# An encoder block on one core: modulation sums spread over the input projection, whose VectorE, ScalarE and GpSimd work runs in written order, and value products of an attention unit in one row

## The chip, the cores and the metric

One core of a Trainium2 chip runs the whole kernel in one launch. The metric is device time in microseconds (us); smaller is better. Below, TensorE (PE) is the matrix engine, VectorE (DVE), ScalarE (ACT) and GpSimd (POOL) work on tiles, and SyncE (SP) issues most DMAs.

## The reference, cut to what matters

A block of 1024 tokens by 1024 channels, float32. Six modulation vectors come from `c`. The mixing half scales and shifts a normalised `x`, multiplies it by one input projection, mixes the first 512 columns with a 2-D Fourier transform, runs windowed attention on the rest (8 query heads, 2 key/value heads, blocks of 128 queries that see the block before, their own and the next one) and projects back. The channel half is a mixture of 16 experts, each on its 128 best tokens.

```python
mod = jnp.einsum('bd,de->be', silu(c), w_ada) + b_ada
sh1, sc1, g1, sh2, sc2, g2 = split(mod, 6)
h = rmsnorm(x, norm_mix_g) * (1.0 + sc1) + sh1
u_f, q, k, v = split(h @ w_in)
q, k = rmsnorm(q, q_norm_g), rmsnorm(k, k_norm_g)
x = x + g1 * (concat([fourier_mix(u_f), windowed_gqa(q, k, v, rel_bias, sink)]) @ w_out)
h2 = rmsnorm(x, norm_ffn_g) * (1.0 + sc2) + sh2
x = x + g2 * expert_choice_moe(h2)
```

## The kernel before, in words

Products are float32 made of three reduced-precision ones: a value is split into a high part (ScalarE copy, L79) and a low part (VectorE subtraction, L80), and TensorE multiplies high by high, low by high and high by low.

**Input projection (L314 to L537).** The 1024 tokens are eight tiles of 128. Tiles 0 and 1 go together while the weights arrive; their order is written out by `in_order(t0, *PINNED)` (L469), which ties each instruction of an engine to the one written before it. Tiles 2 to 7 follow in the loop over `seq` (L493): twelve stages, two for a tile, each of four input chunks. One chunk is `project`: three terms of two or four matmuls (L367). At the head of a stage `chunk` (L258) makes the scaled, transposed and split input of the next stage: four PE transposes (L264), four ScalarE activations (L271, tile `hf`), the split into `hh` (L79) and `hl` (L80). At the head of a tile's first stage also: `scale_x` of the next tile (L222, ScalarE, needs `xr`), and `norm_x` of the tile after that (square on ScalarE L186, a small VectorE operation L187, a power on GpSimd L189 that gives `xr`). Here nothing ties the order of an engine: the compiler's list scheduler orders the instructions by its own estimate of when each is ready.

After a tile's last product `finish` (L374) copies the results out of PSUM (`qn` on VectorE L377; `kk`, `vf`, `un` on ScalarE L378 to L380) and appends the generator `qknorm` (L278) to a list. After each chunk `bg_tick` (L351) advances every `qknorm` by one step: squares (L280, L281), a sum and a scaling on VectorE (L283, L284) and a power on GpSimd (L286, `qr`); two steps later four GpSimd products (L290, L292, L295 twice: `qn`, `kk`, `kd`); four steps later two PE transposes (L302) and a split into `khi` and `klo`.

`bg_tick` also advances `ada_parts` (L140): four of the six modulation vectors, each as eight weighted sums over rows of `w_ada` on VectorE (L114, L116, tile `ws`, one a step), then two matmuls that add over partitions (L174), then a bias (L176); its loads go through SP (L148), its stores through GpSimd's DMA queue (L154). From the second stage on, every other chunk advances it once more (L529), which makes 1.5 steps a chunk. PSUM tiles `pt` (two buffers) serve the chunk transposes, L302 and L174 alike.

**Attention (L540 to L1016).** Sixteen units (tile, key/value head) run through `qprep`, `front` (logits L677 and L678, bias and maximum L680, exponentials L689, division L695) and `back` (L698). `back` handles the unit's two or three key blocks one by one: `flip_p` transposes the probabilities of a block (four PE transposes, L706) and copies them to SBUF (ScalarE L708, tile `pT`, `PB` = 2 buffers); then two value products go into the halves of a PSUM tile (L719, tile `yp`). Each block's transposes are made one block ahead, and between the blocks `tick` advances a filler: first the Fourier group, later the output projection (L74 to L76). The order of all engines is again the list scheduler's.

**Selection and experts (from L1020).** Tokens are chosen on VectorE and TensorE, then the experts' products run back to back, in written order.

Of the kernel before, what the change touches and what calls it, by code (L numbers as in the profile page):

```python
# [30 lines left out]
PINNED = ("PE", "DVE", "Activation", "Pool", "SP")  # L31
RAW1, RAW2, RAW3 = 4, 5, 4
SCRATCH = 4096
SB, PB, WB, YB = 9, 2, 4, 3
OLD = NT - 2
NSW, RATE1, RATE2 = 5, 2.0, 1.3
TK = 3
# [8 lines left out]
def block_kernel(ctx: ExitStack, tc: tile.TileContext, t_in, out):  # L46
    nc = tc.nc
    PE, ACT, DVE, POOL, SP = nc.tensor, nc.scalar, nc.vector, nc.gpsimd, nc.sync
# [7 lines left out]
    def pool(name, bufs=1, space=None, **kw):  # L56
        if space is None:
            return tc.tile_pool(name=name, bufs=bufs, reuse_waits="tile", **kw)
        return tc.tile_pool(name=name, bufs=bufs, space=space, **kw)
# [6 lines left out]
    def pt(name="pt"):  # L66
        return ps.tile([128, 512], F32, name=name, tag="pt", bufs=2)
# [10 lines left out]
    def split(hi, lo, src, eng=None):  # L78
        ACT.activation(hi, src, AF.Copy)  # L79
        return (eng or DVE).tensor_tensor(lo, src, hi.bitcast(F32), op=OP.subtract)  # L80
# [41 lines left out]
    def traced():  # L122
        return len(nc.cur_bb.bb.instructions)

    def in_order(start, *engines):
        last = {}
        for i in list(nc.cur_bb.bb.instructions)[start:]:
            e = str(i.engine).split(".")[-1]
            if e in engines:
                if e in last:  # L130
                    tc.add_manual_dep(i, last[e].name, NOSYNC, reason="program order")
                last[e] = i

    def drain(g):
        for _ in g:
            pass
# [46 lines left out]
    def rms(pool_, src, name, tag, bufs, eng=None):  # L183
        junk = pool_.tile([128, D], BF, name="junk", tag=tag, bufs=bufs)
        ss = pool_.tile([128, 1], F32, name=name + "s", bufs=3)
        ACT.activation(junk, src, AF.Square, accum_out=ss)  # L186
        (eng or DVE).tensor_scalar(ss, ss, 1.0 / D, EPS, op0=OP.mult, op1=OP.add)  # L187
        rs = pool_.tile([128, 1], F32, name=name + "r", bufs=3)
        POOL.tensor_tensor(rs, ss, mhalf[:, 0:1], op=OP.pow)  # L189
        return rs  # L190
# [23 lines left out]
    def load_x(t):  # L214
        xs[t] = p1.tile([128, D], F32, name="xt", bufs=4)
        SP.dma_start(xs[t], x[t * 128:(t + 1) * 128, :])

    def norm_x(t):
        xr[t] = rms(p1, xs[t], "x", tag="hf", bufs=2)

    def scale_x(t):
        ACT.activation(xs[t], xs[t], AF.Copy, scale=xr.pop(t))  # L222
# [53 lines left out]
    px_ = [pt]  # L276

    def qknorm(t, kk):  # L278
        q_n = qn[t]
        ACT.activation(sq[:, 512:], kk, AF.Square)  # L280
        ACT.activation(sq[:, :512], q_n, AF.Square)  # L281
        qs = ust.tile([128, 10], F32, name="qs", bufs=2)
        DVE.tensor_reduce(qs, sq.rearrange("p (h d) -> p h d", d=64), axis=AX.X, op=OP.add)  # L283
        DVE.tensor_scalar(qs, qs, 1.0 / HD, EPS, op0=OP.mult, op1=OP.add)  # L284
        qr = ust.tile([128, 10], F32, name="qr", bufs=2)
        POOL.tensor_tensor(qr, qs, mhalf[:, :10], op=OP.pow)  # L286
        yield
        yield
        qv = q_n.rearrange("p (h d) -> p h d", d=64)
        POOL.tensor_tensor(qv, qv, qr[:, :8, None].to_broadcast([128, 8, 64]), op=OP.mult)  # L290
        kv_ = kk.rearrange("p (h d) -> p h d", d=64)
        POOL.tensor_tensor(kv_, kv_, qr[:, 8:10, None].to_broadcast([128, 2, 64]), op=OP.mult)  # L292
        kd = ust.tile([128, 2, 2, 64], F32, name="kd", bufs=2)
        for dup in range(2):
            POOL.tensor_tensor(kd[:, :, dup, :], kv_, gg[:, None, :].to_broadcast([128, 2, 64]), op=OP.mult)  # L295
        yield
        yield
        yield
        yield
        p = px_[0]()  # L300
        for kv in range(2):
            PE.transpose(p[:, kv * 128:kv * 128 + 128], kd[:, kv].rearrange("p a d -> p (a d)"), ident)  # L302
        split(khi[:, :, t * 128:t * 128 + 128], klo[:, :, t * 128:t * 128 + 128],
              p[:, :256].rearrange("p (a b) -> p a b", b=128))
# [44 lines left out]
    bg, ada, dfts = [], [], []  # L349
# [10 lines left out]
    def terms(ts, kc, hs_, o):  # L360
        for l, r in ((0, w_h), (1, w_h), (0, w_l)):
            for s_ in range(len(ts)):
                lhs = hs_[l][:, o + s_ * 128:o + s_ * 128 + 128]
                for acc, c0, c1 in zip(accs[s_], (0, 512, 1024), (512, 1024, 1280)):

                    first = kc == 0 and l == 0 and r is w_h and not (s_ and c0 == 1024)
                    PE.matmul(acc[:, :c1 - c0], lhs, r[kc][:, c0:c1], start=first, stop=(kc == 7 and r is w_l),  # L367
                              skip_group_check=c0 == 1024)
            yield

    def project(ts, kc, hs_, o):
        drain(terms(ts, kc, hs_, o))
# [79 lines left out]
    pair_products(4, 6)  # L452
    norm_x(2)
    norm_x(3)
    project(pair, 6, hs.pop(6), 0)
    scale_x(2)
    nxt = chunk((2,), 0, 4)
# [32 lines left out]
        folded.append(fold(j, u_n[j], u_n[j + 4]))  # L490

    seq = [(t, kc) for t in range(2, NT) for kc in (0, 4)]
    for m, (t, kc0) in enumerate(seq):  # L493
        hs_ = nxt
        if m == len(seq) - 1:
            for g in ada:
                drain(g)
            p_w.close()
            pfs.append(p_f.enter_context(pool("pf", side="right")))
            for n, wid in ((4, 512), (2, 256), (1, 128), (1, 128)):  # L500
                basis(n, wid)
        if kc0 == 0:
            if t == 2:
                load_x(4)
            if t + 3 < NT:
                load_x(t + 3)
            if t + 1 < NT:
                scale_x(t + 1)
            if t + 2 < NT:
                norm_x(t + 2)  # L510
            accs = [[pu(), pu(), (px, pv)[t % 2]()]]
        if m + 1 < len(seq):
            nxt = chunk((seq[m + 1][0],), seq[m + 1][1], 4)
        for a in range(4):
            project((t,), kc0 + a, hs_, a * 128)
            if m == 0 and a == 1:
                DVE.scalar_tensor_tensor(gg, qg, HD ** -0.5, kg, op0=OP.mult, op1=OP.mult)
                p = pt()
                PE.matmul(p[:8], rb, oh, start=True, stop=True)
                DVE.tensor_tensor(brow, p[:8], brow, op=OP.add)  # L520
            if m == 1 and a == 0:
                SP.dma_start(bd, brow)
            if m == 1 and a == 1:
                SP.dma_start(bd2, bd[None, :, :].to_broadcast([128, 8, 512]))
            if m or a > 1:
                bg_tick()
            if m == len(seq) - 1 and a < 3:
                level0(a)
            if m > 0 and a % 2:  # L529
                next(ada[0], None)  # L530
        if kc0 == 4:
            finish(0, t)
    for g in bg[:-1]:
        drain(g)
    for g in bg[-1:]:
        next(g)
    p_a.close()  # L537


# [158 lines left out]
    def back(t, kv):  # L698
        blocks = span(t)
        sbs = fr.pop((t, kv))  # L700
        yp = ypb()

        def flip_p(bi):
            pp = pt()
            for s_, i in enumerate((0, 2, 1, 3)):
                PE.transpose(pp[:, s_ * 128:s_ * 128 + 128], sbs[i][:, bi * 128:bi * 128 + 128], ident)  # L706
            pT = pb.tile([128, 512], F32, name="pT", bufs=PB)
            ACT.activation(pT, pp, AF.Copy)  # L708
            return pT

        nxt = flip_p(0)
        for bi, b in enumerate(blocks):
            yield
            pT = nxt
            if bi + 1 < len(blocks):
                nxt = flip_p(bi + 1)
            tick()
            for par in range(2):
                PE.matmul(yp[par * 64:par * 64 + 64, :256], vf[:, b, kv * 64:kv * 64 + 64],  # L719
                          pT[:, par * 256:par * 256 + 256], start=(bi == 0), stop=(bi == len(blocks) - 1))  # L720
        ypv = yp[:, :256].rearrange("p (a b) -> p a b", b=128)
        if po is None:
            ya = pb.tile([128, 2, 128], F32, name="ya", bufs=2)
            ACT.activation(ya, ypv, AF.Copy)
            SP.dma_start(yda[t][:, kv * 2:kv * 2 + 2, :], ya)
            ydone[t, kv] = None
        else:
            while ylive[0] >= YB:
                next(fill[0])
            h, l = ysplit(t, kv)  # L730
            split(h, l, ypv)
            ydone[t, kv] = h, l
# [217 lines left out]
    def tick():  # L950
        debt[0] += rate[0]
        while debt[0] >= 1.0:
            debt[0] -= 1.0
            next(fill[0], None)
# [459 lines left out]
```

## Time and profile before

| what | value |
| --- | --- |
| median of 3 runs | 1017.39 us (1016.72 to 1017.52) |
| the profiled execution's own time | 1017.5 us |
| its span, first to last instruction | 1015.4 us |
| TensorE busy | 958.8 us, 94% |
| VectorE, ScalarE, GpSimd busy | 787.4, 628.0, 403.8 us |
| TensorE's share of the chain that ended last | 83% |

The span lies 2.1 us under the execution's own time. Busy time of TensorE is modelled from pipelined records; where an engine stands still, the profile names what ended the wait. In views of stages, the columns give busy time and the number of instructions of each engine, then the mean granted clock of TensorE (1.00 is 2.4 GHz, 0.50 is 1.2 GHz), the share of time in which the DMA engines were busy, and GB/s.

### The profile page before, as it was taken

Reading aid. Unit: us, or ns where it says so; the run is one execution under the profiler, and the core shown is the slowest. Engines: PE = TensorE matmul, PEld = TensorE weight load, DVE = VectorE, ACT = ScalarE, POOL = GpSimd, SP = SyncE. Lnnn points to the kernel's source line nnn. Section 1 sums busy time; section 2 is a strip of 40 time slices with the busy share of each in tenths; the row PEclk is TensorE's granted clock in tenths of the full one; section 3 lists DMA queues with packets and bytes.
Section 4 is the critical chain, followed back from the end, with each engine's and each line's share of the span. In section 5 each row is a group of like instructions: output and inputs, shape, how many; then the busy total and the mean of one; then the engine's idle time right before and its main releaser. Section 6 shows DMA issues by size and latency. Waiting matters only on the chain.

```text
span 1015.4 us, 13138 instructions
## 1 busy us (share of the span) xinstructions
PE 958.8 (94%) x4737; PEld 747.6 (74%) x4737; DVE 787.4 (78%) x1240; ACT 628.0 (62%) x832; POOL 403.8 (40%) x236
## 2 busy tenths in 40 slices
PE   4997999979999999599899999999999999999996
PEld 3676877756777777458788888888888888888884
DVE  1346865777666869779869888988988898899894
ACT  2473444666455553226667777777777777777772
POOL 0026453100000000000357669768776876782203
PEclk9998999989999999599999999999999999999998
DMA  9966664361222138889989999999999999999912
GB/s 292 337 231 248 253 266 126 97 201 53 87 80 73 54 139 304 319 324 352 374 309 385 378 376 411 381 379 399 390 377 379 411 377 380 390 397 379 380 60 41
DMA packets 91641, 283.95 MB, mean 280 GB/s; under 512 B 8140, under 2 KB 25728, under 8 KB 91448
## 3 DMA queue, kind: packets, MB, share of 16 engines
q1 hardware_dynamic: 86712, 266.32, 69.3%
q0 software_dynamic: 4864, 16.80, 6.5%
q8 instruction: 37, 0.61, 0.2%
q14 instruction: 28, 0.23, 0.1%
HBM read 263.79 MB, written 21.40 MB: 281 GB/s over the span
## 4 chain that ended last, share of the span: by engine, by line
PE 83%; DVE 6%; POOL 3%; issue 2%; ACT 2%; DMA 1%; SPq 1%; POOLq 0%; ACTq 0%; DVEq 0%
PE pa L74 17%; PE pa L75 17%; PE pa L76 16%; PE pu L367 5%; PE pt L1258 3%; PE yp L719 3%; PE pj L75 2%; PE pj L74 2%; PE pa L1217 2%; PE pj L76 2%; PE pt L706 2%; PE pt L829 2%; PE lg L677 1%; DVE ws L116 1%; PE lg L678 1%
## 5 line engine op out<-in xcount | busy, mean ns | idle before, releaser
L80 DVE TENSOR_TENSOR wl<-raw,wh 128x2048 fp32r<-128x2048 f32 (+1 forms) x189 | 423.3, 2267 | 64.4 <-ACT wh L79 62.9
L79 ACT ACTIVATE wh<-raw 128x2048 fp32r<-128x2048 f32 (+1 forms) x189 | 355.7, 1895 | 79.0 <-PE pa L75 73.9
L1231 POOL TENSOR_SCALAR oneh<-tri_f,pos 128x128 bf16<-128x128 f32 x96 | 210.3, 2206 | 15.2 <-PE pt L1239 14.9
L74 PE MATMUL pa<-wh,t1h 128*128 128x512 f32 x384 | 152.5, 397 | 0.0
L76 PE MATMUL pa<-wl,t1h 128*128 128x512 f32 x384 | 150.7, 392 | 0.0
L75 PE MATMUL pa<-wh,t1l 128*128 128x512 f32 x384 | 150.6, 392 | 0.0
L74 PE MATMUL pa<-wh,t0h 128*128 128x512 f32 x360 | 144.8, 402 | 0.0
L75 PE MATMUL pa<-wh,t0l 128*128 128x512 f32 x360 | 142.3, 395 | 0.0
L76 PE MATMUL pa<-wl,t0h 128*128 128x512 f32 x360 | 142.2, 395 | 0.0
L792 POOL TENSOR_TENSOR rs<-ss,mhalf 128x1 f32<-128x1 f32 x8 | 4.4, 555 | 221.0 <-DVE ss L790 194.0
L1273 POOL TENSOR_TENSOR ys<-ys,g_r 128x512 f32<-128x512 f32 x30 | 53.5, 1800 | 91.6 <-ACT ys L1272 91.6
L76 PEld LDWEIGHTS pa<-wl,t1h 128*128 128x128 f32 x384 | 72.0, 188 | 16.5
L75 PEld LDWEIGHTS pa<-wh,t1l 128*128 128x128 f32 x384 | 72.1, 188 | 15.6
L74 PEld LDWEIGHTS pa<-wh,t1h 128*128 128x128 f32 x384 | 72.0, 188 | 15.6
L76 PEld LDWEIGHTS pa<-wl,t0h 128*128 128x128 f32 x360 | 68.2, 190 | 15.8
L75 PEld LDWEIGHTS pa<-wh,t0l 128*128 128x128 f32 x360 | 68.3, 190 | 14.9 <-issue 0.2
L74 PEld LDWEIGHTS pa<-wh,t0h 128*128 128x128 f32 x360 | 68.2, 189 | 14.9 <-issue 0.2
L1248 POOL DMA_INDIRECT xe<-h2d,idx x16 | 18.7, 1170 | 150.9 <-DVE gt L1245 150.8
L1276 POOL DMA_INDIRECT out_dram<-ys,idx x16 | 51.1, 3196 | 11.0 <-DVE ys L1275 6.6
L680 DVE CUSTOM_DVE_ANT_0 sb<-lg,bias,sink 128x384 f32<-128x384 f32 (+1 forms) x64 | 35.3, 579 | 16.9 <-PE pt L706 10.6
L367 PE MATMUL pu<-wh,hh 128*128 128x512 f32 x128 | 43.6, 422 | 2.3 <-ACT hh L79 2.1
L708 ACT ACTIVATE pT<-pt 128x512 f32<-128x512 f32 x44 | 25.5, 597 | 32.4 <-PE pt L706 32.2
(311 smaller groups left out, 1647.7 us busy)
## 6 DMA issues: line engine op xcount, KB each, us to landing
raw<-in_w_gate_dram SPq DMA_DIRECT2D x64, 1024.0 KB, 9.7
raw<-in_w_up_dram SPq DMA_DIRECT2D x64, 1024.0 KB, 8.1
raw<-in_w_down_dram SPq DMA_DIRECT2D x63, 1024.0 KB, 8.4
raw<-in_w_ada_dram SPq DMA_DIRECT2D x16, 1024.0 KB, 8.3
raw<-in_w_ada_dram SPq DMA_DIRECT2D x16, 512.0 KB, 8.9
xt<-in_x_dram SPq DMA_DIRECT2D x8, 512.0 KB, 5.0
raw<-in_w_out_dram SPq DMA_DIRECT2D x4, 1024.0 KB
raw<-in_x_dram SPq DMA_DIRECT2D x8, 512.0 KB
```

The costliest lines, as they stand in the source:

```text
L74: PE.matmul(o, lh, rh, start=start, stop=False)
L75: PE.matmul(o, ll, rh, start=False, stop=False)
L76: return PE.matmul(o, lh, rl, start=False, stop=stop)
L79: ACT.activation(hi, src, AF.Copy)
L80: return (eng or DVE).tensor_tensor(lo, src, hi.bitcast(F32), op=OP.subtract)
L367: PE.matmul(acc[:, :c1 - c0], lhs, r[kc][:, c0:c1], start=first, stop=(kc == 7 and r is w_l), skip_group_check=c0 == 1024)
L680: DVE.tensor_tensor_reduce(sb[:, :wid], lg[:, :wid], bias[:, kv * 4 + i, j0:j0 + wid], 1.0, sk[:, i:i + 1], op0=OP.add, op1=OP.max, accum_ ...
L719: PE.matmul(yp[par * 64:par * 64 + 64, :256], vf[:, b, kv * 64:kv * 64 + 64], pT[:, par * 256:par * 256 + 256], start=(bi == 0), stop=(bi ...
L1231: (POOL if t < shared else DVE).tensor_scalar(oneh[:, t, :], slots, pos[:, t, e:e + 1], None, op0=OP.is_equal)
L1258: PE.transpose(p[:, k * 128:k * 128 + 128], src[:, (4 * b + k) * 128:(4 * b + k + 1) * 128], ident)
L1273: POOL.tensor_tensor(ys[:, cs_], ys[:, cs_], g2_r[:, cs_], op=OP.mult)
L1276: POOL.indirect_dma_start(out=out2, out_offset=bass.IndirectOffsetOnAxis(ap=idx[:, :1], axis=0), in_=ys, in_offset=None, compute_op=OP.add)
```

## The change

The extra step of the modulation sums is gone, so they advance one step a chunk. `qknorm` of tile 1 starts four steps later. The load of tile 4's input moves from the loop to the part whose order is written out, so on SP it stands ahead of five small loads. From the loop's start to the end of the projection, VectorE, ScalarE and GpSimd are tied to written order (TensorE and SP are not). In `back`, all transposes and copies of a unit come first, with the same number of ticks, and then all its value products; `pT` gets a third buffer.

```diff
-SB, PB, WB, YB = 9, 2, 4, 3
+SB, PB, WB, YB = 9, 3, 4, 3
...
     def qknorm(t, kk):
+
+        if t == 1:
+            for _ in range(4):
+                yield
         q_n = qn[t]
...
     norm_x(3)
+    load_x(4)
     project(pair, 6, hs.pop(6), 0)
...
     seq = [(t, kc) for t in range(2, NT) for kc in (0, 4)]
+    t1 = traced()
...
         if kc0 == 0:
-            if t == 2:
-                load_x(4)
             if t + 3 < NT:
...
-            if m > 0 and a % 2:
-                next(ada[0], None)
...
     for g in bg[-1:]:
         next(g)
+    in_order(t1, "DVE", "Activation", "Pool")
     p_a.close()
...
-        nxt = flip_p(0)
+
+        pTs = []
+        for bi in range(len(blocks)):
+            pTs.append(flip_p(bi))
+            yield
+            tick()
         for bi, b in enumerate(blocks):
-            yield
-            pT = nxt
-            if bi + 1 < len(blocks):
-                nxt = flip_p(bi + 1)
-            tick()
             for par in range(2):
                 PE.matmul(yp[par * 64:par * 64 + 64, :256], vf[:, b, kv * 64:kv * 64 + 64],
-                          pT[:, par * 256:par * 256 + 256], start=(bi == 0), stop=(bi == len(blocks) - 1))
+                          pTs[bi][:, par * 256:par * 256 + 256], start=(bi == 0), stop=(bi == len(blocks) - 1))
```

## Rows read from the trace of the kernel before

**Rows 1.** Busy time by stage: the loop of the input projection, and attention once the output projection is its filler. Columns: stretch in us, length, busy time (instructions) of PE, weight loads, DVE, ACT, POOL, granted clock, DMA share, GB/s.

```profile
60.00:172.00 112.00, 103.68 (x535) 83.17 (x534) 72.42 (x93) 50.29 (x122) 54.71 (x50) 0.97 0.60 222
220.00:400.00 180.00, 179.62 (x1016) 132.08 (x1015) 133.23 (x460) 95.38 (x266) 4.52 (x9) 0.99 0.30 108
```

**Rows 2.** Who TensorE waited for between 60 and 172 us: us in total, times, longest.

```profile
PE pt L302 <- ACT hf L271: 6.1, 1, 6.1
...
PE pt L174 <- DVE ws L116: 0.4, 1, 0.4
```

**Rows 3.** Busy time in two stretches of 10 us; columns as in the first group.

```profile
80.00:90.00 10.00, 4.19 (x25) 3.40 (x23) 6.10 (x6) 3.38 (x9) 6.59 (x6) 0.87 1.01 359
90.00:100.00 10.00, 9.68 (x41) 7.38 (x42) 6.51 (x10) 2.33 (x7) 3.47 (x2) 0.79 0.44 180
```

**Rows 4.** TensorE in order of time where it stood still: start and length in us, line, tile, count, and in brackets the idle time before and what ended it.

```profile
90.33 0.66 PE L302 MATMUL pt<-ident,kd 128*128 128x128 f32 x2 [6.13 <-ACT hf L271]
```

**Rows 5.** ScalarE in order of time around that place (not all of its rows).

```profile
77.20 0.64 ACT L79 ACTIVATE hh<-hf 128x512 fp32r<-128x512 f32 x1
86.62 1.15 ACT L222 ACTIVATE xt<-xt,xr 128x1024 f32<-128x1024 f32 x1 [8.79 <-POOL xr L189]
...
88.67 1.51 ACT L271 ACTIVATE hf<-pt,sh1c,G1c 128x128 f32<-128x128 f32 x4
```

**Rows 6.** GpSimd in order of time ahead of it (not all of its rows).

```profile
70.43 1.96 POOL L286 TENSOR_TENSOR qr<-qs,mhalf 128x10 f32<-128x10 f32 x1 [2.78 <-DVE qs L284]
...
80.44 4.66 POOL L295 TENSOR_TENSOR kd<-kk,gg 128x128 f32<-128x128 f32 x4
85.06 1.53 POOL L189 TENSOR_TENSOR xr<-xs,mhalf 128x1 f32<-128x1 f32 x1
```

**Rows 7.** ScalarE, copies at the end of tile 3 (the first three) and of tile 7 (the last), four tiles later.

```profile
106.51 0.59 ACT L380 ACTIVATE un<-pu 128x512 f32<-128x512 f32 x1
106.99 0.28 ACT L378 ACTIVATE kk<-pv 128x128 f32<-128x128 f32 x1
107.14 0.29 ACT L379 ACTIVATE vf<-pv 128x128 f32<-128x128 f32 x1
...
170.46 0.60 ACT L380 ACTIVATE u_hi<-pu 128x512 f32<-128x512 f32 x1 [1.02 <-PE pu L367]
```

**Rows 8.** Groups of instructions between 64 and 172 us, shapes kept apart: busy us in total, mean ns of one, idle before.

```profile
L116 DVE SCALAR_TENSOR_TENSOR ws<-raw,c_act,ws 128x1024 f32<-128x1024 f32 x28 | 36.6, 1308 | 0.5
...
L286 POOL TENSOR_TENSOR qr<-qs,mhalf 128x10 f32<-128x10 f32 x7 | 16.3, 2330 | 43.7 <-DVE qs L284 43.7
...
L295 POOL TENSOR_TENSOR kd<-kk,gg 128x128 f32<-128x128 f32 x14 | 14.1, 1029 | 0.4
L80 DVE TENSOR_TENSOR hl<-hf,hh 128x512 fp32r<-128x512 f32 x12 | 10.9, 911 | 15.8 <-ACT hh L79 15.6
L290 POOL TENSOR_TENSOR qn<-qn,qr 128x512 f32<-128x512 f32 x7 | 10.7, 1535 | 0.5
...
L283 DVE TENSOR_REDUCE qs<-ws 128x10 f32<-128x640 f32 x7 | 5.7, 815 | 2.9 <-ACT ws L281 2.9
...
L292 POOL TENSOR_TENSOR kk<-kk,qr 128x128 f32<-128x128 f32 x7 | 5.2, 741 | 0.0
...
L186 ACT ACTIVATE junk<-xt 128x1024 bf16<-128x1024 f32 x4 | 4.3, 1066 | 0.0
```

**Rows 9.** GpSimd, first and last operation of the key and query norm of tile 4 (modulation sums running on VectorE) and of tile 6 (none running).

```profile
126.95 2.52 POOL L286 TENSOR_TENSOR qr<-qs,mhalf 128x10 f32<-128x10 f32 x1 [6.90 <-DVE qs L284]
...
132.53 2.73 POOL L295 TENSOR_TENSOR kd<-kk,gg 128x128 f32<-128x128 f32 x2
...
160.47 1.98 POOL L286 TENSOR_TENSOR qr<-qs,mhalf 128x10 f32<-128x10 f32 x1 [12.04 <-DVE qs L284]
...
164.01 1.66 POOL L295 TENSOR_TENSOR kd<-kk,gg 128x128 f32<-128x128 f32 x2
```

**Rows 10.** SP's issue of the inputs of tiles 4 and 5, and TensorE's first use of the small loads.

```profile
55.40 0.80 SPq L216 DMA_DIRECT2D xt<-in_x_dram  x2
...
72.14 1.02 PE L519 MATMUL pt<-ws,rb 32*8 32x512 f32 x2
```

**Rows 11.** SP's loads of the output projection's weights into the buffers that the modulation sums leave, and ScalarE's first use of them.

```profile
137.68 4.15 SPq L969 DMA_DIRECT2D raw<-in_w_out_dram  x4
...
172.25 1.05 ACT L79 ACTIVATE woh<-raw 128x1024 fp32r<-128x1024 f32 x1
```

**Rows 12.** TensorE in attention, in order of time: four value products between other work, and eight in a row.

```profile
247.39 0.39 PE L75 MATMUL pj<-woh,yl 128*128 128x512 f32 x1
247.62 0.40 PE L76 MATMUL pj<-wol,yh 128*128 128x512 f32 x1
247.95 0.65 PE L719 MATMUL yp<-pT,vf 128*64 128x256 f32 x4
248.53 0.66 PE L706 MATMUL pt<-ident,sb 128*128 128x128 f32 x4
...
372.99 1.08 PE L719 MATMUL yp<-pT,vf 128*64 128x256 f32 x8
```

**Rows 13.** The copies of transposed probabilities over the whole run: count, busy us, mean ns, and the idle time before.

```profile
L708 ACT ACTIVATE pT<-pt 128x512 f32<-128x512 f32 x44 | 25.5, 597 | 32.4 <-PE pt L706 32.2
```

## The prediction, made before the changed kernel was run

> **What bounds the kernel now.** I read the busy time by stage first. In attention from 220 us on TensorE is busy 179.6 of 180 us while VectorE is busy 133.2 and ScalarE 95.4 [rows 1]: whatever TensorE saves there comes off the time. In the projection it is busy 103.7 of 112 [rows 1], so some 8 us are open. The list of its waits puts 6.1 of them on one wait [rows 2], at 84.2 to 90.3 us [rows 4]. The rows of the other engines tell how it came about. TensorE stood at the key transposes, which wanted a PSUM buffer that ScalarE's `hf` had not emptied; ScalarE had put the scaling of tile 5 ahead of `hf` and stood 8.8 us in it [rows 5]; the scaling wanted a power from GpSimd, which came at 85.06, behind the norms of tiles 0 and 1 that had run back to back from 70.43 on [rows 6]. The late power is not needed before tile 5's first chunk, a tile later: the stall is one of order, not of capacity.
>
> It costs more than itself. The granted clock is 0.87 and 0.79 in the two stretches of 10 us around it [rows 3]: 2.6 and 4.2 us at the lower level, 1.2 GHz, which it fell to while TensorE stood. Of the second stretch TensorE still stood 0.33 us, so 3.9 us of work ran at half speed, 1.9 us lost. Stall and clock: 6.13 + 1.9 = **8.0 us**.
>
> What follows attention (selection, experts) starts when attention ends, its weight loads included, so I carry an earlier end through to the end of the run.
>
> **The change, part by part.** *Written order and the late norm of tile 1.* On ScalarE `hf` no longer stands behind a power that is late: between the two norms now lie four chunks, and the power of tile 5 stands on GpSimd after tile 1's `qr` alone, while its user comes two stages later. Gain 8.0.
>
> What the tie adds is waiting behind a late head of a queue. A stage is half of a tile's 16.0 us ((170.46 - 106.51) / 4 [rows 7]), 8.0. After a tile's end ScalarE now runs in this order: `kk`, `vf`, `un` 0.28 + 0.29 + 0.59 [rows 7], scaling 1.15, square 1.07 and its read-out 0.2 (an estimate: the small ones of this trace), `hf` 1.51, `hh` 0.64 [rows 5, 8]: 5.7, then `hl` on VectorE, 0.7 to 0.9: 6.5 us after the tile's end, where the next stage needs it at 8.0. On VectorE the sum for tile t's norm and the weighted sums are queued behind this `hl`, so VectorE stands up to some 4.5 us at each tile's head (from its own copy, about 1, to `hh` at 5.7). Its work of a tile is 72.4 / 6 = 12.1 [rows 1]; 12.1 + 4.5 = 16.6 is just over 16.0, so it arrives at the next tile a little late and the wait shrinks by that: no bound, but no reserve.
>
> The one that waits for it is the key norm. Its reduction ends at 6.5 + 0.82 + 0.2 = 7.5 after the tile's end; GpSimd's chain is 2.33 + 1.54 + 0.74 + 2 x 1.03 = 6.7 [rows 8]: 14.2. TensorE comes to the transposes of `kd` after a stage and three chunks of four: 1.75 x 8.0 = 14.0. With the slowest chain shown (126.95 to 135.26, 8.3 [rows 9]) it is late by 1.8. For tiles 2 to 5 that is 4 x 0.2 to 4 x 1.8, nothing to 7 us. I take 2.5, nearer the mean chain, and 0.5 for the partition sums (L174), which come later with a later VectorE. Projection: -8.0 + 3.0 = **-5.0**, between -8.0 and -0.5.
>
> GpSimd's own row shows what a neighbour costs: 8.3 us for tile 4 beside weighted sums, 5.2 for tile 6 without [rows 9]. The Trainium skill (GPSIMD Engine Reference, Key points) says that GpSimd shares its SBUF interfaces with VectorE and contends with VectorE instructions that have two SBUF inputs, as the weighted sums have; the trace agrees (8.3 against 5.2). The sums, spread until the last tile but one, would by that rule hold every chain at 8.3, and the sum for the projection would be -0.5: a rival below.
>
> *One step a chunk instead of 1.5.* No operation goes. The 41 steps end at the 41st of 46 ticks, in the eleventh of twelve stages. Their buffers go to the output projection's weights, whose loads left at 137.68 and were first used at 172.25 [rows 11], cover of 34 us of which some 15 are used up. Nothing; with the cover gone, a load of some 8 us.
>
> *The moved load.* It left at 55.40 with its neighbour, when tile 0's buffer came free [rows 10], and will still; the five small loads that stand behind it on SP are first used at 72.14 [rows 10], 16 us later. Nothing; without cover, VectorE's first sums would start some us later.
>
> *Value products in a row.* Four records (one block) start at 247.95 and the next work at 248.53: 0.58; the step into them is 0.33 where like work steps by 0.23 [rows 12], 0.10 more. Eight in a row take 1.08 against 0.65 for four, 0.43 more [rows 12]. Joining two blocks saves 0.58 + 0.10 - 0.43 = 0.25 us. There are 44 blocks [rows 13] in 16 units: 28 joints, 7.0 us at most. One joint is there already, and two lie in the two units before 222 us, where TensorE also waits for others: 25 x 0.25 = 6.2. The third `pT` buffer is what keeps the copies ahead of the row: 0.60 us each [rows 13], with two ticks and the next unit's query transposes between the last and the row. Bounds 0 and 7.0; no loss, since the number of transposes, copies and ticks stays. VectorE is 74% busy here, so I let it take a tenth back: **-5.5**.
>
> **Sum.** -5.0 - 5.5 = -10.5 against the profiled execution's own 1017.5, which is the median within 0.1: **1007.0 us**, faster by 1.0%. About 0.2% (2 us) can be told from no change.
>
> **The rivals.** *A. The key norm becomes the wait.* The chain at 8.3 in tiles 2 to 5: 7 us of new waits at L302 on GpSimd's `kd`. For it: the shared interfaces, and VectorE without reserve. Against: three quarters of the chains are shorter, and the scheduler may put the transposes later. 1017.5 - 0.5 - 5.5 = 1011.5. Chance 0.17.
>
> *B. The row does not form.* Attention's order is the scheduler's; if in its reckoning TensorE runs dry it puts a block's product where the gap is, as in the eight that are in a row today. Against: the rows of attention follow written order nearly everywhere. 1017.5 - 5.0 = 1012.5. Chance 0.08.
>
> *C. Slower: the partition sums at their written place.* TensorE is not tied. If L174 stands where it is written, TensorE waits there for the eighth weighted sum, which the tie holds 4.5 us behind at a tile's head. Four parts: 4 x 4.5 = 18, less 8.0 and 5.5: +4.5, 1022. It decides from waits of 3.4 us a part on. Against: with VectorE the busiest, today's L174 waited 0.4 us in all [rows 2], so the scheduler foresees it. Chance 0.08.
>
> *D. New waits eat both gains*, 1017: 0.04.
>
> **The numbers.** My forecast has 0.63, its own range 1003 to 1010.5. Faster: 0.63 + 0.17 + 0.08 = 0.88; same 0.04; slower 0.08. The range goes from all of both terms (1017.5 - 8.0 - 7.0 = 1002.5) to a little past A and B, 1013.5; C and D lie outside.
>
> **What would show it.** Right: no TensorE wait of 6 us in the projection, granted clock 1.00 from 60 to 170 us, L377 of tile 7 about 5 us earlier; the value products as one group of 8 or 12 a unit, their exits to other work 16 in place of 44. Wrong in the first step: waits of TensorE at L302 on GpSimd, at L174 on L116, or at L367 on `hl`, that sum to more than 3 us. Wrong in the second: groups of four, or TensorE idle in attention with VectorE or ScalarE named. Wrong in carrying it on: experts that start earlier and end no earlier, with waits on weight loads.

## The result, and the profile after

The changed kernel takes 1010.44 us (median of 6 runs, 1008.5 to 1011.44), the kernel before 1016.89 in the runs beside it (1016.5 to 1017.52): a ratio of 0.9928 (95% interval 0.9916 to 0.9941), 6.4 us faster. That is 3.4 above the 1007.0 that I had forecast and 0.06 us inside the upper end of the forecast's own range, 1003 to 1010.5. (A ratio, here and below, need not be the quotient of the two medians.) The profiled execution took 1011.29 us, its span 1009.4.

Two landmarks divide the run. ScalarE copies the last accumulator of each tile (L380, now L384); from tile 0's copy to tile 7's is the *loop*. From there to the last copy of transposed probabilities (L708, now L711) is *attention*, and what follows, to the last matmul, is the *rest*. Before: 64.81, 170.46 and 374.92 (the second of two copies in one row), so a loop of 105.6 and 204.5 of attention. After: 65.49, 170.95 and 369.33, so 105.5 and 198.4. **The loop gained 0.2 us where I had put 5.0; attention gained 6.1.** The rest took 630.4 and 630.3.

The rest differs from profile to profile, though no edit below touches its code: 625.8 to 631.3 us over the fourteen profiles of this document. It goes with TensorE's granted clock between 380 and 600 us, which is 0.92 in the three longest (630.3 to 631.3, these two kernels among them) and 0.95 in the five shortest (625.8 to 626.4). Up to 5.5 us of a total can come from there, so an edit to the loop or to attention is read from these stages and not from the median alone.

ScalarE's copies of tiles 0 and 4 and the last copies of attention before; then the copies of tiles 0, 4 and 7 and the last copy of attention after:

```profile
64.81 0.60 ACT L380 ACTIVATE un<-pu 128x512 f32<-128x512 f32 x1
...
122.74 0.60 ACT L380 ACTIVATE u_hi<-pu 128x512 f32<-128x512 f32 x1 [1.02 <-PE pu L367]
...
374.43 1.09 ACT L708 ACTIVATE pT<-pt 128x512 f32<-128x512 f32 x2
```

```profile
65.49 0.60 ACT L384 ACTIVATE un<-pu 128x512 f32<-128x512 f32 x1
...
117.34 0.61 ACT L384 ACTIVATE u_hi<-pu 128x512 f32<-128x512 f32 x1
...
170.95 0.60 ACT L384 ACTIVATE u_hi<-pu 128x512 f32<-128x512 f32 x1
...
369.33 0.60 ACT L711 ACTIVATE pT<-pt 128x512 f32<-128x512 f32 x1 [0.25 <-PE pt L709]
```

Busy time of the stages of [rows 1], after. TensorE is hardly busier in the loop; in attention it holds more instructions in less time.

```profile
60.00:172.00 112.00, 104.36 (x538) 83.21 (x537) 73.59 (x94) 50.58 (x121) 56.34 (x51) 0.98 0.62 216
220.00:400.00 180.00, 176.75 (x1035) 137.01 (x1035) 139.13 (x487) 100.40 (x272) 4.48 (x9) 0.99 0.33 119
```

The wait of [rows 2] on `hf` is gone: ScalarE scales tile 4 in its first 1.2 us after tile 2's copies, with no idle time before it (row of ScalarE, against 8.79 us in [rows 5]). In its place TensorE, in order of time, stands at the partition sums (L174) and at the key transposes (L306, formerly L302), and the clock is down to 0.83 in the stretch from 130 to 140 us:

```profile
83.37 1.17 ACT L222 ACTIVATE xt<-xt,xr 128x1024 f32<-128x1024 f32 x1
```

```profile
114.55 1.05 PE L174 MATMUL pt<-ws,ones 128*32 128x512 f32 x4 [1.10 <-DVE ws L116]
...
132.69 0.49 PE L306 MATMUL pt<-ident,kd 128*128 128x128 f32 x2 [2.62 <-POOL kd L299]
...
152.29 0.44 PE L306 MATMUL pt<-ident,kd 128*128 128x128 f32 x2 [1.54 <-POOL kd L299]
```

```profile
130.00:140.00 10.00, 7.38 (x31) 5.38 (x31) 5.90 (x7) 2.56 (x6) 2.56 (x3) 0.83 0.77 270
```

What TensorE waited for until 132.69 is the norm of tile 4, whose last copy is at 117.34. First VectorE, then GpSimd in order of time:

```profile
122.10 0.69 DVE L80 TENSOR_TENSOR hl<-hf,hh 128x512 fp32r<-128x512 f32 x1 [1.91 <-ACT hh L79]
122.89 0.82 DVE L287 TENSOR_REDUCE qs<-ws 128x10 f32<-128x640 f32 x1
```

```profile
124.00 2.93 POOL L290 TENSOR_TENSOR qr<-qs,mhalf 128x10 f32<-128x10 f32 x1 [3.17 <-DVE qs L288]
126.88 1.08 POOL L154 DMA_DIRECT2D md<-ws  x2
127.97 1.06 POOL L294 TENSOR_TENSOR qn<-qn,qr 128x512 f32<-128x512 f32 x1
128.98 1.40 POOL L296 TENSOR_TENSOR kk<-kk,qr 128x128 f32<-128x128 f32 x1
130.45 2.18 POOL L299 TENSOR_TENSOR kd<-kk,gg 128x128 f32<-128x128 f32 x2
```

The sum starts 5.55 us after the copy, behind `hl`; GpSimd starts at 6.7 and needs 8.6, two DMA issues of 1.08 us among its operations. Before, it started 4.2 us after tile 4's copy (122.74 to 126.95 [rows 9]).

In attention the value products stand in rows of twelve, as the row of TensorE shows (1.52 us, 1.45 to the next work, where three blocks of four cost 3 x 0.58 [rows 12]). In the whole run 46 groups have become 20.

```profile
239.75 0.40 PE L76 MATMUL pj<-wol,yh 128*128 128x512 f32 x1
240.07 1.52 PE L722 MATMUL yp<-pT,vf 128*64 128x256 f32 x12
241.52 0.44 PE L680 MATMUL lg<-khi,qk 128*128 128x384 f32 x1
```

### The profile page after: what moved, and what is told of

Same layout as the page of the kernel before. It is cut to its first block, busy times and chain, and to the rows that moved or that the text cites. A ratio compares the mean times of both kernels' runs of the same rounds, so it can differ in the third digit from the quotient of the medians.

```text
span 1009.4 us, 13146 instructions
## 1 busy us (share of the span) xinstructions
PE 952.2 (94%) x4737; PEld 748.1 (74%) x4737; DVE 788.5 (78%) x1240; ACT 628.2 (62%) x832; POOL 406.8 (40%) x236
## 4 chain that ended last, share of the span: by engine, by line
PE 81%; DVE 7%; ACT 3%; DMA 3%; issue 2%; POOL 2%; SPq 1%; POOLq 0%; ACTq 0%; DVEq 0%
PE pa L74 17%; PE pa L75 17%; PE pa L76 17%; PE pu L371 5%; PE pt L1261 3%; PE pa L1220 2%; PE yp L722 2%; PE pj L75 2%; PE pj L74 2%; PE pj L76 2%; PE pt L709 2%; PE pt L832 2%; PE lg L680 1%; DVE ws L116 1%; DVE wl L80 1%
## 5 line engine op out<-in xcount | busy, mean ns | idle before, releaser
L1234 POOL TENSOR_SCALAR oneh<-tri_f,pos 128x128 bf16<-128x128 f32 x96 | 212.5, 2229 | 15.2 <-PE pt L1242 14.9
L711 ACT ACTIVATE pT<-pt 128x512 f32<-128x512 f32 x44 | 25.9, 596 | 30.5 <-PE pt L709 30.4
```

Source lines behind the costliest of these rows:

```text
L1234: (POOL if t < shared else DVE).tensor_scalar(oneh[:, t, :], slots, pos[:, t, e:e + 1], None, op0=OP.is_equal)
```

## The experiments

Theory: the row brings attention's gain, and the loop lost its own to waits on the key norm. The table has all runs; ratios are against runs of the kernel before on the same chip, loop and attention (us) are from each profiled execution as above, which need not be the median one.

| run | median us (runs) | ratio, 95% interval | loop | attention |
| --- | --- | --- | --- | --- |
| row_alone | 1010.0 (6) | 0.9919, 0.9896 to 0.9942 | 105.4 | 199.7 |
| projection_alone | 1017.24 (12) | 0.9987, 0.9974 to 1.0 | 105.3 | 205.3 |
| buffer_alone | 1018.86 (10) | 1.0006, 0.9985 to 1.0026 | 105.4 | 205.1 |
| kd_later | 1004.81 (4) | 0.9872, 0.9854 to 0.989 | 101.1 | 198.7 |
| keys_first | 1004.2 (4) | 0.9866, 0.9849 to 0.9884 | 100.5 | 198.7 |
| keys_first_later | 1003.45 (5) | 0.9865, 0.9833 to 0.9896 | 100.1 | 198.5 |
| no_sums | 1001.58 (5) | 0.9837, 0.9816 to 0.9857 | 97.9 | 198.5 |
| no_tie | 1005.61 (4) | 0.9876, 0.9848 to 0.9905 | 100.2 | 199.7 |
| faster_sums | 1019.06 (10) | 1.0004, 0.9984 to 1.0024 | 113.2 | 199.9 |
| no_delay | 1010.61 (6) | 0.9937, 0.9917 to 0.9958 | 108.1 | 198.2 |
| delay_and_row | 1005.96 (5) | 0.9884, 0.9861 to 0.9906 | 103.3 | 199.6 |
| spread_and_row | 1009.41 (5) | 0.9914, 0.9892 to 0.9935 | 104.9 | 200.0 |

### Which half of the change brought the time

**row_alone**: the kernel before with `back` and `PB` as in the diff.

> Only the value products in a row, with the third pT buffer; projection as before. Theory: the row alone brings some 5.5 us (25 to 28 joints x 0.25, less what VectorE takes back): 1010.5 to 1012.5. Rival 1 (part of attention's 7 us is a clock fall that was in the execution of before by chance, and the row saves under 3 us): 1014 to 1016. The key transposes of the projection keep their stall of about 6 us on ScalarE's hf in either case.

**projection_alone**: the changed kernel with `back` and `PB` as before.

> The change without the value products in a row (attention as before, two pT buffers). Theory: in the projection the removed stall and clock loss (8.0 us) is taken back by key-norm waits (4.2), a longer wait at the partition sums (0.7) and a new clock fall (1.7); so nearly no change, 1014.5 to 1017.5 us, with waits of TensorE at the key transposes of about 4 us. Rival 1 (the projection brought my forecast 5 us and the row brought little): 1011 to 1013. Rival 2 (the row shortens attention only because the projection's end is put differently): no prediction for this run apart from no gain.

**buffer_alone**: the kernel before with one number changed.

```diff
-SB, PB, WB, YB = 9, 2, 4, 3
+SB, PB, WB, YB = 9, 3, 4, 3
```

> The kernel before with a third pT buffer and nothing else. Theory: TensorE never stood for a pT buffer in attention, so the buffer alone brings nothing: 1016.5 to 1017.5, value products still in groups of four. Rival (the buffer lets the scheduler join blocks by itself): 1011 to 1015, with groups of eight and twelve.

The row alone gives 7.4 us, the projection's part alone nothing that can be told from no change; theory right (the row half a us beyond its range), rival 1 out. Of the row's 7.4 us, 5.1 are in the loop and attention of its profile (0.3 and 4.8); its rest is 2.1 shorter than before, 628.3. The buffer alone gives nothing that can be told, with 46 groups as before; its median is 1.4 us above the range that I expected, and its ten runs reach from 1012.85 to 1021.18. TensorE's waits in the loop, of the row alone and of the projection's part alone:

```profile
PE pt L302 <- ACT hf L271: 6.1, 1, 6.1
```

```profile
PE pt L306 <- POOL kd L299: 4.1, 2, 2.6
PE pt L174 <- DVE ws L116: 1.1, 1, 1.1
```

How much of attention's 6.1 is the row's? The clock has to be the same. Two stretches of attention in the kernel before, in buffer_alone and in row_alone (the clock of the stretches between and behind them is 1.00 in all three):

```profile
200.00:230.00 30.00, 24.30 (x119) 16.90 (x119) 24.79 (x88) 18.98 (x52) 0.00 (x0) 0.89 0.58 178
320.00:340.00 20.00, 19.98 (x102) 14.96 (x102) 14.16 (x50) 10.35 (x30) 0.55 (x1) 0.91 0.20 79
```

```profile
200.00:230.00 30.00, 24.54 (x104) 16.61 (x103) 22.27 (x81) 17.88 (x48) 0.00 (x0) 0.77 0.61 178
320.00:340.00 20.00, 19.98 (x111) 15.05 (x111) 15.09 (x51) 11.86 (x35) 0.55 (x1) 1.00 0.20 79
```

```profile
200.00:230.00 30.00, 24.60 (x103) 16.46 (x103) 22.26 (x82) 17.93 (x50) 0.00 (x0) 0.77 0.60 176
320.00:340.00 20.00, 19.98 (x120) 15.09 (x121) 16.17 (x63) 10.43 (x27) 0.55 (x1) 1.00 0.21 74
```

The last two kernels have the same clock in both stretches, and their attention differs by 205.1 - 199.7 = **5.4 us**: the row's own gain. The remaining 0.7 of the 6.1 I put down to where the half clock fell, by difference and not by a run; the 0.91 around 330 us, in the kernel before alone, has no stand of TensorE beside it, and its cause is open.

### Whether the key norm ate the projection's gain

**kd_later** and **keys_first**, each the changed kernel with one edit in `qknorm`:

```diff
+        yield
+        yield
         p = px_[0]()
```

> The change, with the two key transposes and their split two ticks later (six instead of four steps after the key products). Theory: the 4.2 us of waits on kd go, since GpSimd's chain ends at most 2.6 us after TensorE comes there and two ticks are some 4 us; with them goes the clock fall behind the longest one (1.7). 1010.4 - 4.2 - (0 to 1.7) = 1004.5 to 1006.5. Rival (TensorE has another wait right behind, on hl or on the partition sums, as the tie holds VectorE): 1009 to 1011, with waits at L174 or L371 that grew by 3 us or more.

```diff
-        POOL.tensor_tensor(qv, qv, qr[:, :8, None]..., op=OP.mult)
         POOL.tensor_tensor(kv_, kv_, qr[:, 8:10, None]..., op=OP.mult)
...
             POOL.tensor_tensor(kd[:, :, dup, :], kv_, gg[:, None, :]..., op=OP.mult)
+        POOL.tensor_tensor(qv, qv, qr[:, :8, None]..., op=OP.mult)
```

> The change, with GpSimd's three key products ahead of the query product, at the same ticks. The key chain is then shorter by one query product (1.05 to 1.65 us). Theory: the waits on kd fall from 2.6 and 1.5 to about 1.3 and 0.2, and the clock fall may go: 1006.5 to 1008.5. Rival 1 (the chain's length is set by contention with VectorE, not by its own operations, so that an operation moved away saves nothing): 1009.5 to 1011. Rival 2 (another wait right behind): 1009.5 to 1011, with other waits that grew.

Both confirm it, the second beyond its range. The waits that were left in the loop, of kd_later and then of keys_first, each with its clock:

```profile
60.00:172.00 112.00, 107.16 (x549) 84.20 (x548) 77.53 (x100) 53.70 (x126) 58.64 (x53) 1.00 0.64 220
```

```profile
PE pt L174 <- DVE ws L116: 2.9, 2, 1.7
```

```profile
60.00:172.00 112.00, 107.70 (x548) 84.39 (x549) 78.02 (x101) 55.04 (x128) 59.97 (x52) 1.00 0.64 222
```

```profile
PE pt L306 <- POOL kd L297: 1.6, 1, 1.6
```

With the wait of 2.6 us goes the half clock, and the loop falls by 4.4 and 4.9. (The rest is 3.0 us shorter in both profiles as well, 627.3, so the loop is the measure.) In kd_later a part (2.9 for 1.1) comes back at the partition sums, as its rival had it, but not 3 more.

**keys_first_later**: both ideas, with one `yield` instead of two.

> The change with GpSimd's key products ahead of the query product and the key transposes one tick later. Theory: the wait of 1.6 us on kd that was left in the run with the keys first goes as well: 1002 to 1003.5. Rival (TensorE then waits as long at the next place, the partition sums): 1004 to 1005.

The wait on `kd` is gone, 1.6 us in three parts are left at L174, the loop falls by another 0.4. Its runs reach from 1001.04 to 1009.28, so against keys_first this is no difference that can be told.

### Why GpSimd's chain is late: its start or its length

**no_sums**: in `ada_parts` only the first of eight weighted sums is kept.

```diff
-                    mac(acc, u[:, j:j + 1], 1, 2 * q + j)
+                    if q + j == 0:
+                        mac(acc, u[:, j:j + 1], 1, 2 * q + j)
```

> The change with seven of eight weighted sums of each modulation part left out in the loop (the first of eight stays, so the modulation vectors are not the reference's); everything else as changed. Theory that contention with VectorE's sums stretches GpSimd's chain: it takes 5 to 6 us in place of 8.3, the waits on kd and on the partition sums go, 1003.5 to 1006. Rival (the chain's length is its own): still 8 us a chain; since VectorE has nothing queued the chain may start sooner, the waits on kd shrink to 1 to 3 us, 1005.5 to 1009.

Its norm of tile 4 on GpSimd, and the tile's copy on ScalarE (lines are one further on here):

```profile
122.12 1.96 POOL L291 TENSOR_TENSOR qr<-qs,mhalf 128x10 f32<-128x10 f32 x1 [3.17 <-DVE qs L289]
124.03 1.08 POOL L154 DMA_DIRECT2D md<-ws  x2
125.12 1.06 POOL L295 TENSOR_TENSOR qn<-qn,qr 128x512 f32<-128x512 f32 x1
126.13 0.86 POOL L297 TENSOR_TENSOR kk<-kk,qr 128x128 f32<-128x128 f32 x1
127.07 0.88 POOL L300 TENSOR_TENSOR kd<-kk,gg 128x128 f32<-128x128 f32 x2
```

```profile
115.45 0.60 ACT L385 ACTIVATE u_hi<-pu 128x512 f32<-128x512 f32 x1
```

The chain starts 6.7 us after the copy as in the changed kernel, but takes 5.8 instead of 8.6; no wait is left on `kd` or at L174, and the loop is 97.9. The neighbour on VectorE stretches the chain; the rival (its own length) is out. The time lies under both ranges, for two reasons: `hl` and the partition sums, too, no longer stand behind sums, so the loop's 7.6 us are not all the norm's; and the rest of this profile is 3.0 us shorter, 627.3.

### What the tie, the spread and the delay are worth

**no_tie**:

```diff
-    in_order(t1, "DVE", "Activation", "Pool")
```

> The change without the tie of VectorE, ScalarE and GpSimd to written order. Theory: the tie is what queues the sum of a tile's norm on VectorE behind hl, so that GpSimd's chain starts 6.7 to 7.1 us after a tile's end where before it started 3.7 to 4.6 us after it; without the tie it starts some 2.5 us sooner, and the waits on kd go. If the stall on hf stays away too (tile 1's late norm), the time is 1004 to 1006.5; if the list order brings a stall of its own back, 1010 to 1012, with one wait of 4 to 6 us at L306 on ScalarE. Rival (the chain is late because GpSimd is slow, not because it starts late): waits on kd as with the tie, 1009.5 to 1011.

The time is in the theory's range, but its reason holds by half: the chains of tiles 3, 4 and 5 start 5.2, 7.1 and 4.0 us after the copy, and that of tile 4 is over after 5.9. More telling is ScalarE's row, then TensorE's rows at the old stall:

```profile
87.64 1.15 ACT L222 ACTIVATE xt<-xt,xr 128x1024 f32<-128x1024 f32 x1 [8.80 <-POOL xr L189]
```

```profile
91.26 1.05 PE L174 MATMUL pt<-ws,ones 128*32 128x512 f32 x4 [0.80 <-ACT hf L271]
93.36 0.66 PE L264 MATMUL pt<-ident,xt 128*128 128x128 f32 x4 [1.04 <-DVE klo L80]
```

ScalarE stands for the late power exactly as before, and TensorE waits 1.8 us instead of 6.1. What had stopped it was tile 1's key transposes, in its order ahead of products that had all they needed and asking for a PSUM buffer; the delay puts them four chunks later.

**delay_and_row** and **spread_and_row**: the kernel before with the row, and one of the two.

```diff
+        if t == 1:
+            for _ in range(4):
+                yield
```

> The kernel before with the value products in a row and tile 1's norm four steps later; sums at one and a half steps, no tie, load at its old place. Theory: TensorE stood 6.1 us because tile 1's key transposes were in its order ahead of the chunk's products and wanted a buffer; four steps later they are out of the way, although ScalarE still waits 8.8 us for the power. So 1010.0 (the row alone) less 4 to 6: 1004 to 1006.5. Rival (the delay does nothing by itself; it is the fewer sums that take the stall away): 1009 to 1011, with a wait of 5 to 6 us near 90 us.

```diff
-            if m > 0 and a % 2:
-                next(ada[0], None)
```

> The kernel before with the value products in a row and the modulation sums at one step a chunk; no delay of tile 1's norm, no tie, load at its old place. Theory: the stall at L302 near 90 us does not come from the sums, it stays at 5 to 6 us: 1009 to 1011. Rival (fewer sums let the power come sooner and the stall goes): 1004 to 1006.5.

The spread alone leaves the stall, as its theory has it. The delay alone has the time of its theory, but not its reason in full: the median is 4.0 us under the row's, of which the loop gave 2.1; the rest is 2.4 shorter in its profile, 625.8 against 628.3. Waits of TensorE in the loop, delay first:

```profile
PE pt L174 <- ACT hf L271: 4.3, 1, 4.3
```

```profile
PE pt L302 <- ACT hf L271: 6.1, 1, 6.1
```

With the delay alone, the next work that wants a PSUM buffer takes the place of the transposes: the partition sums, which come early at one and a half steps. Only delay and spread together clear the way (no_tie, which also has the moved load: loop 100.2, against 103.3 and 104.9).

**no_delay** and **faster_sums**: the changed kernel without the delay, and with the extra step of the sums back.

> The change with the norm of tile 1 at its old place (no four steps of delay). Theory: with the tie, the power of tile 4 stands on GpSimd ahead of both norms and its scaling comes two stages later, so the stall does not come back: 1009.5 to 1011.5. Rival (the delay is what takes the stall away; two norms of some 7 us back to back hold GpSimd until 85 us as before): a wait of 4 to 6 us near 85 to 90 us and its clock fall, 1014 to 1018.

> The change with the modulation sums at one and a half steps a chunk again, everything else as changed. Theory: more sums stand on VectorE's tied queue and beside GpSimd's chain in the tiles where TensorE waits already, so the waits grow by 1 to 3 us in tiles 3 and 4 and shrink in tiles 5 and 6, which then have no sums: 1010 to 1013. Rival (spreading the sums costs and brings nothing, as I put it in the prediction): 1009.5 to 1011, with waits on kd unchanged. Rival 2 (the sums are what stretches the chain, so ending them early is better): 1007 to 1009.

Without the delay the time is the theory's, but the loop is 2.6 us longer, with a wait of 1.9 us on `hf`: in part the rival's. (The rest of this profile is 4.5 us shorter than that of the changed kernel, which hides it.) With the extra step the loop is 7.7 us longer, and the time, 1019.06, is far outside all that I expected; its waits, first on the norm, then on `hl` and at the partition sums:

```profile
PE pt L306 <- POOL kd L299: 6.0, 2, 5.0
PE pu L371 <- DVE hl L80: 3.7, 2, 3.4
PE pt L174 <- DVE ws L116: 1.2, 1, 1.2
```

The longest of them, 5.0 us at tile 3's `kd`, is not a longer chain but a later one. Tile 3's copy is at 102.11, so the chain starts 10.2 us after it instead of 6.7, and takes 8.7. ScalarE had stood 3.4 us for TensorE's chunk transposes (L264); why those came late no run shows.

```profile
108.22 1.50 ACT L271 ACTIVATE hf<-pt,sh1c,G1c 128x128 f32<-128x128 f32 x4 [3.44 <-PE pt L264]
```

```profile
112.31 3.02 POOL L290 TENSOR_TENSOR qr<-qs,mhalf 128x10 f32<-128x10 f32 x1 [5.00 <-DVE qs L288]
```

## Why the prediction was right on the whole and wrong in one half

The time lies inside the forecast's range, but the sum behind it does not hold. The loop gave 0.2 us, outside the bounds of its term (0.5 to 8.0), attention 6.1; that the total still fits, by 0.06 us, is luck, and it is nearer to rival A's 1011.5 than to my 1007.0. By the prediction's own sign of a wrong first step, waits on `kd`, at L174 and on `hl` of more than 3 us, that step was wrong: they sum to 5.5 (4.2, 1.1 and 0.2).

**The stall and its clock, 8.0 us: gone, but not for the reason given.** I laid its going to the tie. The tie does clear ScalarE's queue, and without the delay only 1.9 us of wait on `hf` are left. But delay and spread remove most of it with no tie at all. I had traced the stall back to the late power and not asked what TensorE itself stood at, and whether that had to be there.

**New waits, 3.0 us: the step that failed.** They were 4.2 on `kd` and 0.7 more at L174, and they brought a fall of the clock (0.83 in 10 us, so 3.4 us at the lower level and 1.7 lost), which the sum did not have: 6.6 us, with 8.0 against it; some 1.2 us of the balance to the measured 0.2 I cannot place. By terms: the chain's start was predicted 7.5 us after the copy and is 6.7 to 7.1; TensorE's arrival 14.0 and is 12.7 and 13.95 (130.07 and 150.75, where its waits begin, after 117.34 and 136.80); and the chain's length, where I chose "nearer the mean", is 8.3 to 8.6 in each of tiles 3 to 5 (6.0 in tile 2). That is rival A's mechanism (0.17). That its price, 1011.5, is so near to the profiled 1011.3 is chance: A put 7 us on four waits at `kd`, and there were two, of 4.2, with 0.7 at L174 and 1.7 of clock. Its condition stood in the prediction: the sums now lie beside the chains of tiles 3 to 5, so the slow row of [rows 9] was the one to take, not the mean over rows of which some had no sums beside them.

The Trainium skill states (GPSIMD Engine Reference, Key points) that GpSimd contends on its SBUF interfaces with VectorE instructions of two SBUF inputs; the runs agree, with 8.6 us for the chain beside the sums and 5.8 without. It also says (SBUF — State Buffer, "SBUF: two separate sides") that a VectorE instruction with two SBUF inputs and a GpSimd one that reads SBUF take turns, each for its whole instruction; a chain of five operations that is 2.8 us shorter without sums agrees with that, though no run here parts blocking from sharing.

**Spreading the sums, 0: wrong with the tie.** I looked only for who might be late at the end of the sums. Under the tie the spread is worth 7.7 us of loop (faster_sums): with the extra step TensorE waits 3.5 us more on `hl`, which stands in VectorE's queue behind six sums, and 1.8 more on `kd`, where the chain starts later; without the tie and the delay it is worth 0.5 (spread_and_row against row_alone).

**The moved load, 0:** not tried alone. No wait of TensorE names it; VectorE stood 2.2 us for the key norm's weights at 72.2 us, with TensorE at work.

**The row, -5.5: right, 5.4** at equal clock, 0.21 us for each of 26 joints against the 0.25 that I took. Rivals B and C did not come: the rows formed (20 groups, where I had put 16 exits), and L174 cost 1.1.

**Carrying the gain through: right in these two profiles.** From the last copy of attention to the last matmul it is 630.4 and 630.3 us, at the same clock of 0.92 between 380 and 600 us. With 625.8 to 631.3 over all profiles, an agreement to 0.1 is in part luck.

The tie, then, takes back what the other parts of the change give: 105.5 with it, 100.2 without. The prediction's 1007 is about the time of the change without the tie, 1005.61.

## What to carry to other kernels

When a wait is traced back through three engines, look at its near end too: an instruction that stands early in the order of the waiting engine and wants a shared buffer can be moved by one line, whatever makes the buffer late. Tying an engine to written order makes each small operation wait for its predecessor's inputs; before doing so, follow the one chain that runs on the tied engines and has a reader at a fixed place, and price it by the slowest row whose neighbours will be the new neighbours. A stand of TensorE is to be priced with the clock that it costs. And where a long part that no edit touches differs between profiles, as the rest does here, compare the stage that was edited and not the total alone.

## What was not expected of the hardware

GpSimd's operations took longer beside VectorE's weighted sums even where each is small. Means in the loop (groups of instructions, shapes apart), the changed kernel first, then no_sums, whose window takes in one tile more:

```profile
L290 POOL TENSOR_TENSOR qr<-qs,mhalf 128x10 f32<-128x10 f32 x7 | 20.1, 2869 | 31.5 <-DVE qs L288 31.5
L299 POOL TENSOR_TENSOR kd<-kk,gg 128x128 f32<-128x128 f32 x14 | 12.6, 918 | 0.5
```

```profile
L291 POOL TENSOR_TENSOR qr<-qs,mhalf 128x10 f32<-128x10 f32 x8 | 17.2, 2156 | 39.3 <-DVE qs L289 39.3
L300 POOL TENSOR_TENSOR kd<-kk,gg 128x128 f32<-128x128 f32 x16 | 9.6, 623 | 0.6
```

A power of ten elements a partition loses 0.7 us, a product of 128 elements 0.3. And TensorE's stand of 2.62 us was followed by 1.2 GHz at once (clock 0.97 from 132 to 133 us, 0.50 from 133 to 136), where kd_later and keys_first, with stands up to 1.7 us, kept 1.00 in the loop.
